# A store cut into pieces of 7, 70, 10, 40 and 1 rows, and VectorE's copies of V on later iterations

## The chip, the cores and the metric

The kernel runs on one core of one Trainium2 chip. The metric is the device time of one execution in microseconds (us). Times of a kernel are medians of several runs; a profile is one further execution, whose own time is given beside its span (first to last instruction of the program).

## The reference

Attention over 8 x 12 = 96 heads of 512 rows and 64 columns, float32 in and out. Each row attends to itself and to its ancestors in a binary tree whose node i has the parent (i - 1) // 2; everything else is masked.

```python
scores = np.einsum('bhqd,bhkd->bhqk', Q, K) * scale
scores = scores + (1 - mask) * (-1e9)
weights = np.exp(scores - np.max(scores, axis=-1, keepdims=True))
weights = weights / (np.sum(weights, axis=-1, keepdims=True) + 1e-10)
return np.einsum('bhqk,bhkd->bhqd', weights, V)
```

Q, K and V are 12.58 MB each, and so is the output.

## The kernel before

**Tiles.** The 96 heads are worked off in 48 pairs, one pair per iteration `i` of the loop at line 746 (49 iterations: the values and the division of pair `i - 1` run in iteration `i`). For a pair, TensorE transposes K and Q (`turn`, lines 427 and 459 for the wide form used from pair 8 on), VectorE copies the transposes out of PSUM (438, 442, 446 for K, 467 for Q; two pairs at a time, K in odd iterations and Q in even ones), TensorE makes the scores (`scores1`, `scores2`; the tree mask comes in as extra products with `codes`), ScalarE takes the exponential (502, 533), TensorE multiplies with V (`values`, 578), and VectorE takes the reciprocal of the sums (608) and multiplies (610) into the output tile `of`. In the wide form, the Q of pair `j` is transposed some two iterations before iteration `j`, its K some three.

**Loads.** Q, K and V come from HBM by DMAs that GpSimd (POOL) issues and that cast float32 to bf16. K and Q come in DMAs of up to 8 heads (`load_k`, `load_q`; line 253). V comes in groups of 16 heads: `load_rows` (line 282) brings 64 or 32 of the 128 partitions, `load_leaves` (line 291) brings the leaf rows of 8 heads to 32 partitions. Heads 48 to 63 are V's group 3, 64 to 79 group 4, 80 to 95 group 5.

**Copies of V.** Before V can be multiplied, its rows are copied within SBUF into `vt`, in the order of the tree (`spread`, the copy itself at line 361). There are two sets of `vt`, used by the groups in turn. The parts "A", "B", "C", "E" of groups 3 to 5 are the leaves and are copied by VectorE; "M" and "Y" of group 2 too; "X", "N", "Z0", "Z1" and the parts 6 to 9 (`spread_top`) of these groups are copied by POOL. Which engine copies what in which iteration is written out by hand: `BY_VECTOR` and `BY_SCALAR` by iteration, and from group 4 on `STEADY_VECTOR`, one copy in each iteration of the group before. The copy stands last in its iteration's work on VectorE. POOL's copy of "X" in group 2 needs VectorE's "M" of the same heads to have come first.

**Stores.** The output is stored from `of`, in tiles of 16 heads (`VO`): each of 128 partitions holds 1 KB for each head. Stores of heads 0 to 87 are issued by POOL, those of the last heads by SyncE (SP) and ScalarE (line 619 all).

**The order on POOL.** `pool_program` is one list of loads, copies and stores that POOL goes through in this order; `ready` only says from which iteration of the loop an entry may be emitted. Each DMA that POOL issues has one of eight semaphores in turn, and waits for the landing of the DMA that had it before, eight DMAs earlier in the list.

Of the kernel before, what the change touches and what calls it, by code (L numbers as in the profile page):

```python
# [119 lines left out]
def kernel(  # L120
# [7 lines left out]
    nc = tc.nc  # L128
    B, H, S, D = Q.shape
    P = nc.NUM_PARTITIONS  # L130
    assert S == 512 and D == 64 and P == 128 and (B * H) % 4 == 0
    scale = float(1.0 / np.sqrt(D))
    NH = B * H
# [3 lines left out]
    KB, VB, VO = 8, 16, 16  # L137
# [342 lines left out]
    def scores1(i):  # L480

        sp = psS.tile([P, 2, 512], fp32, name="s1")
        for a in range(2):
            nc.tensor.matmul(  # L484
                out=sp[:, a, :],
                lhsT=(k1code if i < WIDE else k1wide)[64 * a:64 * a + CODE_ROWS, :],
                rhs=(q1code[64 * a:64 * a + CODE_ROWS, :] if i < WIDE
                     else q1wide[64 * a:64 * a + CODE_ROWS, :, :]),
                start=True, stop=False,
            )  # L490
        for a in range(2):
            nc.tensor.matmul(  # L492
                out=sp[:, a, :], lhsT=keys(i, a, TOP),
                rhs=qTs[i][64 * a:64 * a + 64, :, :].rearrange("p t c -> p (t c)"),
                start=False, stop=True,
            )
        et = etpool.tile([P, 2, 4, 128], bf16, name="e1")
        nc.scalar.activation(  # L498
            out=et[:, :, :, :].rearrange("p a t c -> p (a t c)"),
            in_=sp[:, :, :].rearrange("p a c -> p (a c)"),  # L500
            func=AF.Exp, scale=scale,
        ) if i < WIDE else nc.scalar.activation(  # L502
            out=et[:, :, :, :].rearrange("p a t (r u) -> p a (t r) u", u=2),
            in_=sp[:, :, :].rearrange("p a (u c) -> p a c u", u=2),
            func=AF.Exp, scale=scale,
        )
        ets[i] = et
# [109 lines left out]
    def store(eng, h0, n, step=1, p0=0, p1=P):  # L617
        g, f = divmod(h0, VO)
        return eng.dma_start(  # L619
            out=Or[p0:p1, h0:h0 + step * (n - 1) + 1:step, :],  # L620
            in_=ofs[g][p0:p1, f:f + step * (n - 1) + 1:step, :, :].rearrange(
                "p h t d -> p h (t d)"
            ),
        )

    def pool_program():

        ops = [
            (load_k, 2, 2), (load_q, 2, 2), (load_v, 0, 4), (load_v, 4, 4),
            (load_k, 4, 2), (load_k, 6, 2), (load_q, 4, 2), (load_k, 8, 4),  # L630
            (load_q, 6, 2), (load_q, 8, 4), (load_v, 8, 8), (load_k, 12, 4),
            (load_q, 12, 4), (load_k, 16, 4), (load_rows, 1, "upper"),
            (load_q, 16, 4), (load_rows, 1, "even"), (load_k, 20, 4), (load_rows, 1, "odd"),
            (load_q, 20, 4), (load_k, 24, 8), (load_q, 24, 4), (load_rows, 2, "upper"),
            (load_q, 28, 4), (load_k, 32, 4), (load_rows, 2, "even", "odd"),
            (load_q, 32, 8), (load_k, 36, 4), (load_rows, 3, "upper"),
            (spread_pool, (1, "Z0", 8, 16), (1, "Z1", 8, 16)),
            (load_k, 40, 8), (load_q, 40, 8), (load_leaves, 3, 0), (load_leaves, 3, 1),
            (spread_top, 2, 0, 16), (spread_pool, (2, "Z0", 0, 16), (2, "Z1", 0, 16)),
            (load_q, 48, 8), (spread_pool, (2, "X", 0, 8)),  # L640
            (load_k, 48, 8), (spread_pool, (2, "X", 8, 16)),
            (load_rows, 4, "upper"), (spread_top, 3, 0, 16),
            (load_k, 56, 8), (load_q, 56, 8), (load_leaves, 4, 0), (load_leaves, 4, 1),
            (spread_pool, (3, "X", 0, 16), (3, "N", 0, 16), (3, "Z0", 0, 16), (3, "Z1", 0, 16)),
            (load_k, 64, 8), (load_q, 64, 8), (store, nc.gpsimd, 0, 16),
            (load_k, 72, 8), (spread_top, 4), (load_q, 72, 8),
            (spread_pool, (4, "X", 0, 16), (4, "N", 0, 16)),
            (load_rows, 5, "upper"), (spread_pool, (4, "Z0", 0, 16), (4, "Z1", 0, 16)),
            (load_leaves, 5, 0), (load_leaves, 5, 1), (load_k, 80, 8), (load_q, 80, 8),
            (store, nc.gpsimd, 16, 8), (load_k, 88, 8), (load_q, 88, 8),  # L650
            (store, nc.gpsimd, 24, 8), (store, nc.gpsimd, 32, 16),
            (spread_top, 5), (spread_pool, (5, "X", 0, 16), (5, "N", 0, 16)),
            (store, nc.gpsimd, 48, 16), (spread_pool, (5, "Z0", 0, 16), (5, "Z1", 0, 16)),
            (store, nc.gpsimd, 64, 8), (store, nc.gpsimd, 72, 8), (store, nc.gpsimd, 80, 8),
        ]
        return ops

    def ready(op, i):

        f, args = op[0], op[1:]  # L660
        if f in (load_k, load_q):
            return 2 * (i + 3) >= args[0] + args[1] - 4 * KB
        if f is load_v:
            return True
        if f in (load_rows, load_leaves):
            return 2 * i >= VB * (args[0] - 2)
        if f is spread_pool:
            tops = [(("vt", "M", VB * o + h) in issued) for o, part, h0, h1 in args if part == "X"
                    and o < EIGHT for h in range(h0, h1)]
            return 2 * i >= VB * (args[0][0] + 1 - NV) and all(tops)  # L670
        if f is spread_top:
            return 2 * i >= VB * (args[0] + 1 - NV)
        return 2 * i >= args[1] + args[2]

    BY_VECTOR = {
# [20 lines left out]
    }  # L696
    BY_SCALAR = {
# [8 lines left out]
    }  # L706

    STEADY_VECTOR = {
        0: [("A", 0, 8)], 1: [("B", 0, 8)], 2: [("C", 0, 8)], 3: [("E", 0, 8)],
        4: [("A", 8, 16)], 5: [("B", 8, 16)], 6: [("C", 8, 16)], 7: [("E", 8, 16)],  # L710
    }

    def spread_by(copy, table, steady, i):

        o, j = divmod(i, 8)
        todo = table.get(i, [])
        if 4 <= o + 1 < NH // VB:
            todo = todo + [(o + 1,) + piece for piece in steady.get(j, [])]
        for args in todo:
            spread(copy, *args)  # L720

    program = pool_program()

    def pool(i):
# [21 lines left out]
    for i in range(NP + 1):  # L746
        steps = FIRST[i] if i < len(FIRST) else "SVK" if i % 2 else "SVQ"
        for step in steps:
            if step == "S" and i < NP:
                scores1(i)  # L750
                scores2(i)
            if step == "V" and i >= 1:
                values(i - 1)
                norm(i - 1)
                valued = True
            if step == "K" and kdone < NP:
                kdone = turn("kst", kdone)
            if step == "Q" and qdone < NP:
                qdone = turn("qst", qdone)
            if step == "W":  # L760
                nc.scalar.copy(
                    out=codes[64:64 + CODE_ROWS, 1280:1536], in_=codes[0:CODE_ROWS, 1280:1536]
                )
            if step == "X":
                spin("s1" if valued else "ob", 2)
            if step == "D":
                spread_by(nc.vector.tensor_copy, BY_VECTOR, STEADY_VECTOR, i)
            if step == "A":
                spread_by(nc.scalar.copy, BY_SCALAR, {}, i)
        if "D" not in steps:  # L770
            spread_by(nc.vector.tensor_copy, BY_VECTOR, STEADY_VECTOR, i)
        if "A" not in steps:
            spread_by(nc.scalar.copy, BY_SCALAR, {}, i)
        pool(i)
        if i >= NP - 3 and i < NP:
            store(nc.sync, head(i - 1, 0), 2, 2)
# [33 lines left out]
```

## Time and profile before

| what | value |
| --- | --- |
| median of 3 runs | 135.08 us (134.81 to 135.19) |
| the profiled execution | 135.36 us |
| its span | 133.6 us |
| busy: PE, VectorE (DVE), ScalarE (ACT), POOL | 113.5, 108.0, 94.4, 73.5 us |
| DMAs issued by POOL, SP and ACT | 60, 6 and 3 |
| mean granted TensorE clock | 0.971 |

The profile's page shows each engine's busy time, the span in 40 slices (a slice here is 3.34 us; digits are tenths), the DMA queues, a chain of waits followed back from the last instruction, groups of instructions by line, and the DMA issues. Further views list an engine's instructions in order of time (start, length, engine, line, operation, output and inputs, shapes, count, and in brackets the idle time before it with what ended it), and the busy time of each engine in chosen stretches (from:to, length, then PE, PEld, DVE, ACT, POOL with instruction counts, then the granted clock, the mean busy share of the sixteen DMA engines, and GB/s). A DMA engine can have several packets open at once, so its share can be over 1. q0 is the queue of POOL's DMAs, q1 and q10 those of SP and ACT, q8 and q14 carry instructions. "DMA x<-y" as a releaser means that an engine waited for a DMA to land.

### The profile page before, as it was taken

The page shows a single profiled execution, that of the slowest core. Times are in us where ns is not written, and L with a number is a line of the kernel's source. Part 1 is how long each engine was busy: PE and PEld are TensorE (multiplying, and loading weights), DVE is VectorE, ACT ScalarE, POOL GpSimd, SP SyncE. Part 2 cuts the span into 40 slices and gives each one's busy share as a digit, 9 for nine tenths or more (in the row PEclk, how much of TensorE's full clock was granted, in tenths as well). Part 3 has the DMA queues.
Part 4 walks back from the last instruction along what each step waited for, and adds up shares of the span by engine and source line. Part 5 has one row for each costly group of instructions (what it writes and reads, how often), then busy time and mean ns, then how long its engine had stood idle before and what let it go on. Part 6 is the DMA issues. An engine that isn't in the chain of part 4 may idle for free.

```text
span 133.6 us, 5525 instructions
## 1 busy us (share of the span) xinstructions
PE 113.5 (85%) x2414; PEld 78.6 (59%) x2417; DVE 108.0 (81%) x261; ACT 94.4 (71%) x153; POOL 73.5 (55%) x98
## 2 busy tenths in 40 slices
PE   6887959999799799898899799999678998989910
PEld 2444646677577567575577567777456665666610
DVE  3349766888999999999999999995999998857440
ACT  4369575889769769686877858778567788696900
POOL 6999525364286996999705998223999302002000
PEclk9999995999999999999999999999999999999985
DMA  2999999999999999999999999999999999999980
GB/s 94 230 195 194 200 196 202 200 201 207 198 204 204 200 205 205 205 205 202 205 206 210 215 380 330 211 199 205 208 326 242 286 405 400 402 399 393 382 288 30
DMA packets 30232, 32.29 MB, mean 242 GB/s; under 512 B 1104, under 2 KB 27344, under 8 KB 30208
## 3 DMA queue, kind: packets, MB, share of 16 engines
q0 software_dynamic: 28352, 30.15, 113.0%
q1 hardware_dynamic: 1296, 1.33, 2.9%
q10 hardware_dynamic: 560, 0.46, 1.4%
q8 instruction: 19, 0.31, 0.9%
q14 instruction: 5, 0.04, 0.1%
HBM read 37.96 MB, written 12.58 MB: 378 GB/s over the span
## 4 chain that ended last, share of the span: by engine, by line
PE 30%; DVE 30%; DMA 18%; POOL 11%; issue 5%; ACT 2%; ACTq 0%; DVEq 0%; POOLq 0%
PE ob L578 11%; DVE of L610 10%; DMA vst<-in_V_dram 10%; DVE vt L361 8%; DMA kst<-in_K_dram 8%; PE s L484 4%; POOL vt L361 4%; DVE rec L608 3%; PE s L492 3%; DVE kq L467 3%; PE qtp L459 3%; PE ktp L427 3%; POOL kst L241 2%; POOL qst L241 2%; DVE kq L438 2%
## 5 line engine op out<-in xcount | busy, mean ns | idle before, releaser
L502 ACT ACTIVATE e<-s 128x1024 bf16<-128x1024 f32 x40 | 40.9, 1023 | 22.0 <-PE s L492 21.3
L578 PE MATMUL ob<-vt,e 128*128 128x65 bf16 (+1 forms) x940 | 37.4, 198 | 8.8 <-DVE of L610 5.8
L578 PEld LDWEIGHTS <-e 128*128 128x128 bf16 (+1 forms) x960 | 30.6, 103 | 17.8 <-DVE of L610 7.7
L533 ACT ACTIVATE e<-s 128x384 bf16<-128x384 f32 x80 | 34.7, 491 | 0.0
L610 DVE TENSOR_TENSOR of<-ob,rec 128x512 f32<-128x512 f32 x47 | 32.5, 691 | 1.6
L361 POOL COPY vt<-vst 32x512 int32<-32x512 int32 (+1 forms) x34 | 28.0, 823 | 7.6 <-PE ob L578 5.4
L361 DVE COPY vt<-vst 32x1024 bf16<-32x1024 bf16 (+6 forms) x54 | 26.3, 486 | 4.6 <-DMA vst<-in_V_dram 3.7
L484 PE MATMUL s<-codes 40*128 40x512 bf16 x96 | 19.3, 398 | 0.8 <-ACT e L498 0.4
L619 POOL DMA_DIRECT2D out_dram<-of x8 | 8.0, 997 | 20.1 <-DVE of L610 16.0
L492 PE MATMUL s<-kq 64*128 64x512 bf16 x96 | 18.5, 382 | 0.0
L608 DVE RECIPROCAL rec<-ob 128x8 f32<-128x8 f32 x47 | 9.6, 204 | 8.2 <-PE ob L578 7.6
L527 PEld LDWEIGHTS <-kq 64*128 64x128 bf16 x320 | 12.3, 94 | 5.6 <-issue 0.5
L527 PE MATMUL s<-kq 64*128 64x160 bf16 (+1 forms) x320 | 14.8, 208 | 0.3 <-issue 0.3
L517 PE MATMUL s<-codes 40*128 40x384 bf16 x80 | 13.6, 334 | 0.3
L467 DVE COPY kq<-qtp 128x1024 bf16<-128x1024 bf16 x20 | 13.6, 680 | 0.0
L427 PE MATMUL ktp<-ptile,kst 128*64 128x128 bf16 x320 | 12.5, 219 | 0.7 <-DVE kq L446 0.3
L498 ACT ACTIVATE e<-s 128x1024 bf16<-128x1024 f32 x8 | 8.2, 1022 | 6.3 <-PE s L492 6.3
L253 POOL DMA_DIRECT2D kst<-in_K_dram x12 | 9.0, 751 | 6.4 <-DMA kst<-in_K_dram 3.2
L459 PE MATMUL qtp<-ptile,qst 128*64 128x128 bf16 x320 | 12.3, 219 | 0.0
L253 POOL DMA_DIRECT2D qst<-in_Q_dram x12 | 8.8, 736 | 5.1 <-PE ob L578 2.1
L282 POOL DMA_DIRECT2D vst<-in_V_dram x9 | 6.8, 760 | 7.4 <-DMA vst<-in_V_dram 6.0
L517 PEld LDWEIGHTS <-codes 40*128 40x128 bf16 x80 | 5.8, 94 | 8.6 <-issue 1.3
(43 smaller groups left out, 124.3 us busy)
## 6 DMA issues: line engine op xcount, KB each, us to landing
out_dram<-of POOLq DMA_DIRECT2D x3, 2048.0 KB, 21.1
out_dram<-of POOLq DMA_DIRECT2D x5, 1024.0 KB, 17.0
kst<-in_K_dram POOLq DMA_DIRECT2D x8, 512.0 KB, 14.0
qst<-in_Q_dram POOLq DMA_DIRECT2D x8, 512.0 KB, 15.6
vst<-in_V_dram POOLq DMA_DIRECT2D x12, 256.0 KB, 13.7
vst<-in_V_dram POOLq DMA_DIRECT2D x6, 512.0 KB, 13.5
kst<-in_K_dram POOLq DMA_DIRECT2D x6, 256.0 KB, 11.9
qst<-in_Q_dram POOLq DMA_DIRECT2D x6, 256.0 KB, 12.2
```

What stands on the lines that cost most here:

```text
L253: return nc.gpsimd.dma_start(out=kept[b][:, h0 % KB:h0 % KB + n, :, :].rearrange("p (g x) t d -> p g (x t d)", x=2), in_=wide[:, h0 // 2:( ...
L361: return copy(out=dst, in_=src)
L427: nc.tensor.transpose(out=columns(kp[64 * a:64 * a + 64, :], mixed, (256, 2), (leaves - mixed, 2), (1, 32)), in_=st[:, 2 * i % KB // 2 + a ...
L467: nc.vector.tensor_copy(out=qq[:, :, 0:16, :].rearrange("p b u c -> p b (u c)"), in_=halves)
L484: nc.tensor.matmul(out=sp[:, a, :], lhsT=(k1code if i < WIDE else k1wide)[64 * a:64 * a + CODE_ROWS, :], rhs=(q1code[64 * a:64 * a + CODE_ ...
L492: nc.tensor.matmul(out=sp[:, a, :], lhsT=keys(i, a, TOP), rhs=qTs[i][64 * a:64 * a + 64, :, :].rearrange("p t c -> p (t c)"), start=False, ...
L502: ) if i < WIDE else nc.scalar.activation(
L517: nc.tensor.matmul(out=flat[:, a, :, :].rearrange("p u (t c) -> p u t c", t=4)[:, :, :, 16:64], lhsT=k2wide[64 * a:64 * a + CODE_ROWS, :], ...
L527: nc.tensor.matmul(out=flat[:, a, :, lo:hi], lhsT=keys(i, a, WTILE2[t]), rhs=qT[64 * a:64 * a + 64, :, lo:hi], start=False, stop=t == 1, s ...
L533: nc.scalar.activation(out=e2s[i % NE][:, a, :, 32:128].rearrange("p t (r u) -> p t r u", u=2), in_=flat[:, a, :, :].rearrange("p u (t r) ...
L578: nc.tensor.matmul(out=ob[lo:hi, a, 65 * t:65 * t + 65], lhsT=e[:, a, PLACE[t], lo:hi], rhs=vt[vtile[tile_v][0]][:, head(i, a) % VB, vtile ...
L610: nc.vector.tensor_tensor(out=ofs[g][:, first:last + 1:step, :, :], in0=o4[:, a:a + n, :, 0:D], in1=rec[:, a:a + n, :, :].to_broadcast([P, ...
```

## The change

`store_rows` cuts the store of heads 0 to 15 by partitions into five DMAs: rows 0 to 6, 7 to 76, 77 to 86, 87 to 126, and 127 (7, 70, 10, 40 and 1 rows of 16 heads each). The first two are issued between the loads of K and Q of heads 64 to 71, the third behind that load of Q, the last two behind POOL's copies 6 to 9 of group 4. Before, the whole store stood behind the load of Q of heads 64 to 71.

VectorE's copies of the leaves of groups 3, 4 and 5 are put in one table, one per iteration, from iterations 19, 27 and 35 on (before: group 3 two in each of the iterations 18, 20, 22, 24, groups 4 and 5 one per iteration from 24 and 32 on). In group 2, the two copies "M" and the first "Y" change places: "M" of heads 32 to 39 in iteration 13 (was 12), "Y" of the same in 14 (was 15), "M" of heads 40 to 47 in 15 (was 14). The number of copies stays. On POOL four DMAs are added.

```diff
+    DEALT = (0, 7, 77, 87, 127, P)
+
+    def store_rows(j0, j1):
+
+        for j in range(j0, j1):
+            store(nc.gpsimd, 0, VO, 1, DEALT[j], DEALT[j + 1])
+
     def pool_program():
...
-            (load_k, 64, 8), (load_q, 64, 8), (store, nc.gpsimd, 0, 16),
-            (load_k, 72, 8), (spread_top, 4), (load_q, 72, 8),
+            (load_k, 64, 8), (store_rows, 0, 2), (load_q, 64, 8), (store_rows, 2, 3),
+            (load_k, 72, 8), (spread_top, 4), (store_rows, 3, 5), (load_q, 72, 8),
...
+        if f is store_rows:
+            return 2 * i >= VO
...
-        12: [(2, "M", 0, 8)],
-        14: [(2, "M", 8, 16)],
-        15: [(2, "Y", 0, 8)],
+        13: [(2, "M", 0, 8)],
+        14: [(2, "Y", 0, 8)],
+        15: [(2, "M", 8, 16)],
         16: [(2, "Y", 8, 16)],
-        18: [(3, "A", 0, 8), (3, "B", 0, 8)],
-        20: [(3, "C", 0, 8), (3, "E", 0, 8)],
-        22: [(3, "A", 8, 16), (3, "B", 8, 16)],
-        24: [(3, "C", 8, 16), (3, "E", 8, 16)],
     }
+    for o, start in ((3, 19), (4, 27), (5, 35)):
+        for j in range(8):
+            h0 = VB // 2 * (j // 4)
+            BY_VECTOR[start + j] = [(o, "ABCE"[j % 4], h0, h0 + VB // 2)]
...
-    STEADY_VECTOR = {
-        0: [("A", 0, 8)], 1: [("B", 0, 8)], 2: [("C", 0, 8)], 3: [("E", 0, 8)],
-        4: [("A", 8, 16)], 5: [("B", 8, 16)], 6: [("C", 8, 16)], 7: [("E", 8, 16)],
-    }
-
-    def spread_by(copy, table, steady, i):
-
-        o, j = divmod(i, 8)
-        todo = table.get(i, [])
-        if 4 <= o + 1 < NH // VB:
-            todo = todo + [(o + 1,) + piece for piece in steady.get(j, [])]
-        for args in todo:
+    def spread_by(copy, table, i):
+
+        for args in table.get(i, []):
             spread(copy, *args)
```

More of the change, by code (lines that the diff above doesn't have):

```diff
@@ L766 @@
             if step == "D":
-                spread_by(nc.vector.tensor_copy, BY_VECTOR, STEADY_VECTOR, i)
+                spread_by(nc.vector.tensor_copy, BY_VECTOR, i)
             if step == "A":
-                spread_by(nc.scalar.copy, BY_SCALAR, {}, i)
+                spread_by(nc.scalar.copy, BY_SCALAR, i)
         if "D" not in steps:
-            spread_by(nc.vector.tensor_copy, BY_VECTOR, STEADY_VECTOR, i)
+            spread_by(nc.vector.tensor_copy, BY_VECTOR, i)
         if "A" not in steps:
-            spread_by(nc.scalar.copy, BY_SCALAR, {}, i)
+            spread_by(nc.scalar.copy, BY_SCALAR, i)
         pool(i)
```

## The prediction

> **What bounds the kernel now.** I read the page first (the slices by tenths, the DMA queues), then the busy time by stretches at the end, VectorE's timeline, and last the completion events of single DMAs.
>
> ```profile
> span 133.6 us, 5525 instructions
> DVE  3349766888999999999999999995999998857440
> DMA  2999999999999999999999999999999999999980
> GB/s 94 230 195 194 200 196 202 200 201 207 198 204 204 200 205 205 205 205 202 205 206 210 215 380 330 211 199 205 208 326 242 286 405 400 402 399 393 382 288 30
> q0 software_dynamic: 28352, 30.15, 113.0%
> q8 instruction: 19, 0.31, 0.9%
> q14 instruction: 5, 0.04, 0.1%
> HBM read 37.96 MB, written 12.58 MB: 378 GB/s over the span
> ```
>
> The DMA row stands at 9 from the second slice to the last but one: the sixteen DMA engines have work queued all the time, and the rate (a load counts its bf16 side here, so 205 GB/s is 410 read) moves little. The bytes are fixed. What can still differ is which engine ends last. The end:
>
> ```profile
> 126.00:127.00 1.00, 0.93 (x22) 0.67 (x21) 0.62 (x2) 0.92 (x3) 0.00 (x0) 1.00 1.00 377
> 129.50:130.00 0.50, 0.00 (x0) 0.00 (x0) 0.00 (x0) 0.00 (x0) 0.00 (x0) 0.50 0.83 289
> 130.00:130.50 0.50, 0.00 (x0) 0.00 (x0) 0.00 (x0) 0.00 (x0) 0.00 (x0) 0.50 0.34 105
> 130.50:131.00 0.50, 0.00 (x0) 0.00 (x0) 0.00 (x0) 0.00 (x0) 0.00 (x0) 0.50 0.21 68
> 131.00:131.50 0.50, 0.00 (x0) 0.00 (x0) 0.00 (x0) 0.00 (x0) 0.00 (x0) 0.50 0.20 70
> 131.50:132.00 0.50, 0.00 (x0) 0.00 (x0) 0.00 (x0) 0.00 (x0) 0.00 (x0) 0.50 0.06 21
> 128.75 0.35 ACTq L619 DMA_DIRECT2D out_dram<-of  x1
> ```
>
> The last but one column is the DMA share: 0.20 of sixteen is about three engines, alone at work from 130.5 to nearly 132. The last store is issued at 128.75. So the end is set by three late engines. Why they are late shows in the sixteen completion events that each DMA leaves, one for each engine (my own listing of the trace; the first column is the issue):
>
> ```
>  42.39 V leaves 3   55.9 56.2 56.3 56.4 56.4 56.4 56.8 56.9 57.4 57.4 57.4 57.5 57.6 57.6 57.6 57.9
>  51.30 V 4 upper    63.7 63.8 64.0 64.0 64.1 64.5 64.7 64.8 65.1 65.1 65.2 65.2 65.2 65.3 65.3 65.4
>  55.36 K 56 to 63   66.2 66.4 66.5 66.6 66.6 67.1 67.1 67.3 67.6 67.7 67.7 67.7 67.8 67.8 67.9 69.3
>  56.11 Q 56 to 63   68.7 68.9 69.1 69.1 69.1 69.6 69.7 69.8 70.2 70.2 70.2 70.3 70.4 70.4 70.5 71.4
>  62.61 K 64 to 71   73.8 74.0 74.2 74.2 74.3 74.7 74.8 74.9 75.3 75.3 75.3 75.4 75.5 75.5 76.5 76.6
>  63.36 Q 64 to 71   76.4 76.6 76.7 76.7 76.8 77.2 77.3 77.5 77.9 77.9 77.9 77.9 78.0 78.1 79.1 79.2
>  64.10 store 0-15   81.8 81.9 82.0 82.0 82.1 82.4 82.5 82.7 83.0 83.0 83.1 83.2 83.3 84.3 84.4 84.6
> 121.55 store 80-87 125.9 126.0 126.1 126.2 126.2 126.3 126.6 127.1 127.7 127.7 128.0 128.1 128.2 128.3 129.6 129.7
> 127.30 store 92,94 129.2 129.2 129.2 129.2 129.3 129.3 129.3 129.4 129.7 129.7 130.0 130.0 130.1 131.2 131.3 131.6
> 128.75 store 95    130.3 130.3 130.3 130.3 130.3 130.3 130.4 130.4 130.4 130.4 130.6 130.6 130.8 131.8 132.0 132.2
> ```
>
> Eight engines have fallen back by about 1.3 us at 65 us; then one, two and three of them fall back by another 1.1. The 19 instruction pieces of queue q8 explain it: 0.31 MB in 19 is 16 KB each, 0.9% of 16 engines x 133.6 us is 19 us, so 1.0 us on one engine each. Nineteen over eight engines in turn is two for each and a third for three of them. The other eight get none (a few have one of the short q14 pieces). That it is always the same eight is inferred from the steps in these rows.
>
> The computing ends beside this, and has one hole:
>
> ```profile
> 90.71 0.69 DVE L610 TENSOR_TENSOR of<-ob,rec 128x512 f32<-128x512 f32 x1
> 91.32 0.68 DVE L467 COPY kq<-qtp 128x1024 bf16<-128x1024 bf16 x1
> 93.64 0.62 DVE L361 COPY vt<-vst 32x1024 bf16<-32x1024 bf16 x1 [1.64 <-DMA vst<-in_V_dram]
> 96.11 0.85 DVE L361 COPY vt<-vst 32x1024 bf16<-32x1024 bf16 x1
> 98.55 0.92 DVE L361 COPY vt<-vst 32x1024 bf16<-32x1024 bf16 x1
> 101.44 0.42 DVE L361 COPY vt<-vst 32x1024 bf16<-32x1024 bf16 x1
> 103.46 0.67 DVE L361 COPY vt<-vst 32x1024 bf16<-32x1024 bf16 x1
> 95.41 4.96 POOL L361 COPY vt<-vst 32x512 int32<-32x512 int32 x6
> 101.52 2.33 POOL L361 COPY vt<-vst 32x1024 int32<-32x1024 int32 x2
> 111.07 0.69 DVE L610 TENSOR_TENSOR of<-ob,rec 128x512 f32<-128x512 f32 x1
> 112.72 0.21 DVE L608 RECIPROCAL rec<-ob 128x8 f32<-128x8 f32 x1 [0.36 <-PE ob L578]
> 124.77 0.69 DVE L610 TENSOR_TENSOR of<-ob,rec 128x512 f32<-128x512 f32 x1
> ```
>
> From 31 us VectorE hardly idles except for 1.64 us before 93.64, in front of the first copy of the V leaves of group 5; its copies take 0.62 to 0.92 beside POOL's copies and 0.42 alone. From 112 us it waits for PE.
>
> **The change, part by part. The store of heads 0 to 15.** One DMA of 128 rows is eight rows on each engine. Its 2.10 MB at about 401 GB/s (slices of 405, 400, 402) are 5.23 us, so 0.65 us for a row on one engine; the rows of Q 64 and of the store say the same (medians 77.7 and 82.85). The new pieces of 7, 70, 10, 40 rows don't divide by 16. No DMA of this kernel has such a number of rows, so how they fall is bounded. One end is an even spread by their 1 KB runs: eight rows' worth each, nothing moves. The other is whole rows on as many engines as divide the number, each piece starting where the last one stopped: 7 engines x 1, 14 x 5, 10 x 1, 10 x 4, and the last row in sixteen 1 KB runs. Counted from the first engine: places 0 to 4, 7 and 8 get ten rows, place 15 nine, places 5, 6 and 9 to 14 six. I take this end, because it splits the engines into eight that get more and eight that get less, as the rows above do, and four rows, 2.6 us, are near the 2.4 to 2.8 us between the first and the last engine there. The trace doesn't name the engines: whether the eight with six rows are the eight late ones is open, and is the first rival.
>
> Where they agree, the three last engines lose two rows: 132.24 - 1.31 = 130.9. The eight early ones gain two. They end 121.55's store at 125.9 to 127.1, and had they been kept fed, five more stores of 256, 256, 256, 128 and 128 KB (2.6 us at 401 GB/s) would end at 128.5 to 129.7; plus 1.31 is 129.8 to 131.0. The five in between come to 128.3 + 2.6 - 1.3 = 129.6. So the queue ends near 130.95 in place of 132.24: **-1.3 us**. Dealt without any rest, the mean over the engines, (8 x 129.0 + 5 x 130.6 + 3 x 132.1)/16 = 130.1, is the floor: -2.1 us.
>
> The Trainium skill ("DMA: Bandwidth & Descriptors", the section on why a DMA increments its semaphore by 16) states a division like the end I take: the largest number of engines up to 16 that divides the rows, then consecutive engines from a cursor. It also notes an exception, a sixteenth of the rows rounded up on each engine from the first, which is the second rival below. No run here shows either yet.
>
> **Four more DMAs on POOL, and three loads moved.** POOL's rows around them, and two of VectorE's:
>
> ```profile
> 51.30 0.83 POOL L282 DMA_DIRECT2D vst<-in_V_dram  x1
> 50.26 0.42 DVE L361 COPY vt<-vst 128x1024 bf16<-128x1024 bf16 x1
> 52.84 0.77 DVE L361 COPY vt<-vst 64x1024 bf16<-64x1024 bf16 x1
> 62.61 0.76 POOL L253 DMA_DIRECT2D kst<-in_K_dram  x1
> 63.36 0.75 POOL L253 DMA_DIRECT2D qst<-in_Q_dram  x1
> 64.10 1.18 POOL L619 DMA_DIRECT2D out_dram<-of  x1
> 65.92 0.75 POOL L253 DMA_DIRECT2D kst<-in_K_dram  x1 [0.64 <-PE s L492]
> 71.44 2.69 POOL L361 COPY vt<-vst 32x512 int32<-32x512 int32 x4 [4.77 <-PE ob L578]
> 74.09 0.74 POOL L253 DMA_DIRECT2D qst<-in_Q_dram  x1
> 80.18 1.15 POOL L291 DMA_DIRECT2D vst<-in_V_dram  x2
> 70.00:80.00 10.00, 8.93 (x206) 6.37 (x204) 9.64 (x23) 7.38 (x13) 8.21 (x10) 1.00 1.19 267
> ```
>
> Each issue costs POOL 0.58 (a load of 32 rows, two in 1.15) to 1.18; five in place of one are 1.7 to 4.7 us more, say 2.5. POOL idles 4.77 us before 71.44, which takes that. Each DMA also waits for the eighth one before it, so with four more in the row Q 64 to 71 goes out near 66 (behind V 4, 65.4), K 72 near 72 (Q 56, 71.4), Q 72 near 77 (K 64, 76.6), and the leaves of group 5, four copies later, near 83.5 in place of 80.18. Behind POOL then are its copies for group 4, wanted by PE at about 95. On the engines nothing runs dry: Q 64, issued at 63.36, lands at 76 to 79, so some 12 us lie queued, and the window has a share over 1. Cost 0; without that cover 2.5 to 3.3 us. Q 64 lands behind 77 rows of the store, 3.1 us later, at about 82; its transposes run two iterations before the copy of 91.32, near 87.
>
> The Trainium skill ("DMA: Bandwidth & Descriptors", "Rules for kernel authors") speaks against this: large DMAs of 128 partitions, small ones merged; with the 2.0 us of its fit ("Anatomy of one DMA") four more would cost 8 us, and the sum be 141.8, if they stood in line. The share over 1 says that they overlap instead.
>
> **VectorE's copies.** The same number, later: group 4 starts at iteration 27 (was 24), group 5 at 35 (was 32), each still ahead of the values of its heads (33 and 41). The 1.64 us wait goes, since iteration 35 is about 7 us later and the leaves have long landed. Four copies no longer run beside POOL: (0.62 + 0.85 + 0.92 + 0.67) - 4 x 0.42 = 1.38. Three copies of 0.42 move past 112 us into VectorE's gaps there. Together at most 4.3 us; the eight iterations between the L610 rows of 90.71 and 111.07 take 20.4, while the six from there to 124.77, where VectorE waits for PE, take 2.28 each; at that pace eight take 18.2, so about 2.1 is had, or 0 if PE gives nothing back. In group 2 one copy for POOL comes an iteration later (from 50.3 to 52.8), which moves the load of 51.30 by some 3 us, under the same backlog: 0. What is late next: the stores. Earlier computing feeds engines that are already fed, so its own worth at the end is **0** while the three late engines set it; it makes sure that the early ones don't rest after 127 us (share 0.67 there now).
>
> ```profile
> 127.00:128.00 1.00, 0.48 (x12) 0.32 (x10) 0.71 (x3) 0.00 (x0) 0.00 (x0) 1.00 0.67 245
> SPq L805 <- DMA out_dram<-of: 3.5, 1, 3.5
> ```
>
> **Sum.** The span's 133.6 less 1.3 is 132.3. The profiled execution took 135.36, so 1.76 lies around its span: 134.1. It stands 0.28 above the median of 135.08: **133.8 us**.
>
> **The rivals.** *The rows fall on the wrong engines* (slower): if one of the three late engines has ten rows, it ends at 132.24 + 1.31 = 133.55, and the whole at 136.4; with nine, 135.7. It decides from more than eight rows on any of the three. For it: nothing in the trace ties a row to an engine, and a blind fit is unlikely. Against it: the counts and the size match. *Rounded up from the first engine* (slower): pieces of 1, 5, 1 and 3 rows an engine give ten rows to seven engines, nine to three, eight to three, six to one, none to two; the three late ones then most likely have eight to ten: 135.1 to 136.4, say 135.9. *An even spread* (the change doesn't do what it says): the three late engines end at 132.2 as before, the computing's 2.1 us vanish behind them: 135.0. *Half a fit*, where the late ones lose one row: 134.4, which I count with the forecast.
>
> **How the numbers follow.** Forecast 0.60, wrong engines 0.22, rounded up 0.08, even spread 0.10. The three runs shown lie within 0.28%, so 0.3% (0.4 us) is about what can be told from no change. The forecast's own range is 133.0 (the floor) to 134.6; the slower cases reach 136.5. From 133.1 to 136.5 some 0.15 is left out. Faster 0.60, same 0.10, slower 0.30.
>
> **What would show it.** In the profile after: the DMA share in the last microsecond before the end falls from many engines at once, not in a step to three; the sixteen events of the DMAs after 82 us lie within about 1.5 us, where they lay 2.8 apart; no wait of VectorE for V at 93 us; the last copies at 0.42 and PE done near 125. Wrong would be a spread over 4 us after the store, a wait of VectorE or PE for Q 64, or a DMA share under 0.9 between 65 and 85 us.

## The result, and the profile after

| kernel | median | range, runs | ratio to before (95%) | profiled execution | its span |
| --- | --- | --- | --- | --- | --- |
| before | 135.08 us | 134.78 to 135.5, 10 | 1 | 135.36 us | 133.6 us |
| changed | 136.03 us | 135.53 to 137.16, 10 | 1.0079 (1.005 to 1.0109) | 136.0 us | 134.2 us |

The changed kernel is slower by 0.8%, where 133.8 us and faster was forecast. In the experiments a ratio is to the kernel before run beside it on the same chip (medians of 135.0 to 135.37 us). An execution more than 1.5% above the fastest of its kernel is left out of the ratios: one of 139.26 us of the pieces alone, and one of 146.06 us at a granted clock of 0.668 of the whole store issued earlier, which is also that kernel's only profile, so that of it only the times are used.

The page of the changed kernel, the lines that answer to those of before:

```profile
span 134.2 us, 5529 instructions
DVE  3439779888999899959999999898988999774400
DMA  4999999999999999999999999999999999999971
GB/s 132 212 176 195 199 196 200 201 202 206 200 201 203 202 204 206 206 207 201 209 202 211 311 247 243 255 221 201 207 311 257 278 382 402 403 404 398 401 284 48
q0 software_dynamic: 28624, 30.15, 113.4%
q8 instruction: 19, 0.31, 0.8%
```

The DMA row is the same as before, 9 from the second slice on, to the last but two. The hump of the store in the GB/s row (380, 330 before) is now spread over 311, 247, 243, 255. Nothing in these lines looks like a loss. It shows in the completion events (own listing: the issue, the first, the mean and the last of the sixteen events):

```
                       before                         changed
K 64 to 71   62.61  73.81  75.02  76.61     63.91  73.96  75.00  76.34
Q 72 to 79   74.09  86.77  88.05  89.94     76.82  86.63  88.96  92.50
Q 80 to 87   82.07  97.05  98.41  99.93     87.72  97.85  99.40 102.38
store 80-87 121.55 125.94 127.37 129.66    118.66 126.58 129.06 132.23
SP's last   128.20 129.71        131.93    125.31 128.49        133.32
ACT's last  128.75 130.29        132.24    125.86 128.84        132.59
```

Up to K 64 to 71, the last load ahead of the store, the two kernels agree within 0.3 us. Between it and Q 72 to 79 lie the same bytes in both (Q 64 to 71, the store of heads 0 to 15, K 72 to 79, Q 72 to 79). Before they took the sixteen engines 13.03 us on the mean, changed 13.96; and the engines lie 5.9 us apart behind them, where it was 3.2. The 2.6 us that the last engine loses (89.94 to 92.50) are still there at the store of heads 80 to 87 (129.66 to 132.23). The end, in stretches (the columns as in the prediction):

```profile
128.00:129.00 1.00, 0.00 (x0) 0.00 (x0) 0.00 (x0) 0.00 (x0) 0.00 (x0) 0.50 0.97 346
129.00:130.00 1.00, 0.00 (x0) 0.00 (x0) 0.00 (x0) 0.00 (x0) 0.00 (x0) 0.50 0.80 292
130.00:131.00 1.00, 0.00 (x0) 0.00 (x0) 0.00 (x0) 0.00 (x0) 0.00 (x0) 0.50 0.43 155
131.00:132.00 1.00, 0.00 (x0) 0.00 (x0) 0.00 (x0) 0.00 (x0) 0.00 (x0) 0.50 0.29 101
132.00:133.00 1.00, 0.00 (x0) 0.00 (x0) 0.00 (x0) 0.00 (x0) 0.00 (x0) 0.50 0.12 43
```

The share still falls in steps, to two engines in the last full microsecond, where it was to fall for many at once. The computing did end earlier, as the rows of VectorE, SP and ACT in order of time show:

```profile
91.39 0.69 DVE L610 TENSOR_TENSOR of<-ob,rec 128x512 f32<-128x512 f32 x1
93.09 0.42 DVE L361 COPY vt<-vst 32x1024 bf16<-32x1024 bf16 x1
95.41 0.70 DVE L361 COPY vt<-vst 32x1024 bf16<-32x1024 bf16 x1
97.99 0.40 DVE L361 COPY vt<-vst 32x1024 bf16<-32x1024 bf16 x1
123.87 0.73 PE L578 MATMUL s<-vt,e 128*64 128x65 bf16 x14
125.86 0.35 ACTq L619 DMA_DIRECT2D out_dram<-of  x1
```

No wait for V stands at 93 us, the copies take 0.40 to 0.42 but for one, PE ends at 124.6 and the last store is issued at 125.86 (before 128.75). And POOL's rows:

```profile
63.91 0.76 POOL L253 DMA_DIRECT2D kst<-in_K_dram  x1
64.67 1.62 POOL L619 DMA_DIRECT2D out_dram<-of  x2
66.47 0.79 POOL L253 DMA_DIRECT2D qst<-in_Q_dram  x1 [0.19 <-issue]
69.33 0.62 POOL L619 DMA_DIRECT2D out_dram<-of  x1 [2.07 <-DMA kst<-in_K_dram]
71.78 0.78 POOL L253 DMA_DIRECT2D kst<-in_K_dram  x1 [1.84 <-PE qtp L459]
75.42 1.41 POOL L619 DMA_DIRECT2D out_dram<-of  x2
76.82 0.82 POOL L253 DMA_DIRECT2D qst<-in_Q_dram  x1
82.91 0.59 POOL L291 DMA_DIRECT2D vst<-in_V_dram  x1
```

The five pieces take 1.62 + 0.62 + 1.41 = 3.65 where one took 1.18. So the pieces went out when they were to, the computing gained what it was to, and the DMA engines, busy all the time, did the same bytes in more time.

### The profile page after: what moved, and what is told of

The parts are those of the page before. It is cut to its first block, busy times and chain, and to the rows that moved or that the text cites. A ratio compares the mean times of both kernels' runs of the same rounds, so it can differ in the third digit from the quotient of the medians.

```text
span 134.2 us, 5529 instructions
## 1 busy us (share of the span) xinstructions
PE 113.0 (84%) x2414; PEld 78.6 (59%) x2417; DVE 106.6 (79%) x261; ACT 94.5 (70%) x153; POOL 76.4 (57%) x102
## 3 DMA queue, kind: packets, MB, share of 16 engines
q0 software_dynamic: 28624, 30.15, 113.4%
## 4 chain that ended last, share of the span: by engine, by line
PE 30%; DMA 30%; POOL 15%; DVE 11%; issue 5%; ACT 2%; ACTq 0%; POOLq 0%; DVEq 0%
DMA vst<-in_V_dram 16%; DMA qst<-in_Q_dram 13%; PE ob L578 10%; POOL vt L361 6%; PE s L484 5%; DVE vt L361 4%; PE qtp L459 3%; PE ktp L427 3%; DVE of L610 3%; PE s L492 3%; PE s L527 3%; PE s L517 2%; POOL kst L241 2%; POOL qst L241 2%; ACT e L533 1%
## 5 line engine op out<-in xcount | busy, mean ns | idle before, releaser
L361 DVE COPY vt<-vst 32x1024 bf16<-32x1024 bf16 (+6 forms) x54 | 24.7, 458 | 3.7 <-DMA vst<-in_V_dram 2.7
L619 POOL DMA_DIRECT2D out_dram<-of x12 | 10.4, 872 | 15.4 <-DVE of L610 10.4
L459 PE MATMUL qtp<-ptile,qst 128*64 128x128 bf16 x320 | 12.8, 220 | 1.5 <-issue 1.3
```

The source lines that it names most:

```text
L361: return copy(out=dst, in_=src)
L459: nc.tensor.transpose(out=halves[64 * a:64 * a + 64, :, c:c + 64], in_=st[:, 2 * i % KB // 2 + a, 4 * u + t, :], identity=ptile[:, 0:128],)
```

## The experiments

**The two parts alone.** First the new copies of VectorE with the store whole, then the pieces with the old copies.

```diff
 vec_only, against the changed kernel
-            (load_k, 64, 8), (store_rows, 0, 2), (load_q, 64, 8), (store_rows, 2, 3),
-            (load_k, 72, 8), (spread_top, 4), (store_rows, 3, 5), (load_q, 72, 8),
+            (load_k, 64, 8), (load_q, 64, 8), (store, nc.gpsimd, 0, 16),
+            (load_k, 72, 8), (spread_top, 4), (load_q, 72, 8),
 store_only: BY_VECTOR, STEADY_VECTOR and spread_by as before
```

> VectorE's copies moved as in the change, the store of heads 0 to 15 whole as before. Theory (the uneven pieces cost the time, through the DMA engine that ends last): the three late engines still end near 132.2 us, so 135.1 us (ratio 0.998 to 1.002), although the last store is issued 2 to 3 us earlier (near 126). Rival (moving the copies is what costs): 136.0 us, ratio 1.005 or more.

> The store cut into 7, 70, 10, 40 and 1 rows, VectorE's copies as before. Theory: about the changed kernel's time, 135.5 to 137.2 with the same wide scatter from run to run (ratio about 1.008), and completion events of one DMA up to 4 to 6 us apart after 82 us. Rival (moving the copies costs): 135.1 us.

Measured: VectorE's copies alone 134.76 us, ratio 0.9981 (0.9956 to 1.0006); the pieces alone 137.47 us, 1.0158 (1.0108 to 1.0209). From K 64 to Q 72 the mean is 13.07 and 14.14 us (13.03 before, 13.96 changed). The loss is the pieces'. VectorE's part is worth 0.3 us or nothing with the whole store, and about 1.1 us with the pieces (by the ratios, 1.0158 against 1.0079). In the run of the pieces alone the computing ends last, after one wait of 4.2 us of VectorE for V's leaves (until 95.84, when the slowest engine had brought them at 95.82):

```profile
DVE vt L361 <- DMA vst<-in_V_dram: 6.7, 4, 4.2
132.20 0.36 ACTq L619 DMA_DIRECT2D out_dram<-of  x1
```

**Even cuts.** The first theory was the dealing itself: whole rows in unequal numbers on the engines. Cut at 16, 80, 96 and 112 rows, every piece divides by 16 and each engine gets eight rows in all, as from the whole store.

```diff
-    DEALT = (0, 7, 77, 87, 127, P)
+    DEALT = (0, 16, 80, 96, 112, P)
```

> The changed kernel with the five pieces cut at 16, 80, 96, 112 (16, 64, 16, 16, 16 rows): five DMAs at the same places on POOL, but every one divides evenly over sixteen engines. Theory: 135.0 us (ratio 0.996 to 1.002), events after 82 us at most 3 us apart, little scatter. Rival (the five issues, their waits and the later loads cost): 136.0 us with the same scatter as the changed kernel.

Measured: 136.29 us, ratio 1.0088 (1.0057 to 1.0119), as slow as the changed kernel, and the mean from K 64 to Q 72 is 14.55 us, more than its 13.96. That theory fell. The time is that of the rival, that the five issues and the moved loads cost, which the cut by heads below puts to the test.

**A probe of the dealing.** The store of heads 32 to 47 was issued by SyncE in pieces of 64, five times 8, four times 4 and four times 2 rows, which was to name the engines.

```diff
-            (store, nc.gpsimd, 24, 8), (store, nc.gpsimd, 32, 16),
+            (store, nc.gpsimd, 24, 8),
...
+        if i == 24:
+            row = 0
+            for n in (64,) + (8,) * 5 + (4,) * 4 + (2,) * 4:
+                store(nc.sync, 32, 16, 1, row, row + n)
+                row += n
+            assert row == P
```

> A probe on the kernel before: heads 32 to 47 are stored from SyncE in one DMA of 64 rows, five of 8, four of 4 and four of 2, so that engines fixed by number get 4, 9, 13 and 17 rows (8, 4, 2 and 2 engines) if a piece of 8, 4 or 2 rows goes to that many lowest-numbered engines. Then the sixteen events of the next load fall in four sets 3.3, 2.6 and 2.6 us apart, and within each set the engines that carry the instruction pieces stand 1.2 to 2.4 us behind: this counts how many of the eight late engines are among numbers 0 to 1, 2 to 3, 4 to 7 and 8 to 15. If the late eight are not fixed engines, or pieces are spread evenly, no such sets appear. Time some 140 us, of no interest.

Measured: one execution, 141.9 us (span 140.1). The events of later loads lie up to 12 us apart, and they do fall in sets of 8, 4, 2 and 2: those of the load of Q issued at 95.82 us lie from 107.7 to 110.3, from 112.8 to 114.5, at 116.4 and 117.0, and at 118.7 and 119.8. This is what whole rows, on as many engines as the piece has rows, were to give. The means of the sets are 4.4, 2.9 and 2.6 us apart, where 3.3, 2.6 and 2.6 had been expected. How many of the late engines are in each set can't be read from them, so the question for the engines' names stays open. With some 140 us expected from the uneven dealing alone, the time speaks for no theory.

**Cut by rows in one place, cut by heads in five.** Two things were still mixed: that the store is cut by rows, and that it stands between loads in five places.

```diff
 together and even_together, against vec_only
-            (load_k, 64, 8), (load_q, 64, 8), (store, nc.gpsimd, 0, 16),
+            (load_k, 64, 8), (load_q, 64, 8), (store_rows, 0, 5),
 by_heads, against vec_only
-            (load_k, 64, 8), (load_q, 64, 8), (store, nc.gpsimd, 0, 16),
-            (load_k, 72, 8), (spread_top, 4), (load_q, 72, 8),
+            (load_k, 64, 8), (store, nc.gpsimd, 0, 1), (store, nc.gpsimd, 1, 9), (load_q, 64, 8),
+            (store, nc.gpsimd, 10, 1),
+            (load_k, 72, 8), (spread_top, 4), (store, nc.gpsimd, 11, 4), (store, nc.gpsimd, 15, 1),
+            (load_q, 72, 8),
 whole_earlier, against vec_only
-            (load_k, 64, 8), (load_q, 64, 8), (store, nc.gpsimd, 0, 16),
+            (load_k, 64, 8), (store, nc.gpsimd, 0, 16), (load_q, 64, 8),
```

> The changed kernel, with its five pieces of 7, 70, 10, 40 and 1 rows issued one after the other where the whole store stood (behind Q 64 to 71, ahead of K 72 to 79); VectorE's copies as in the changed kernel. Theory (turns: the DMA engines lose about 0.2 to 0.3 us each time the work changes between loads and a store, and the changed kernel has six such places where there were two): the cut alone costs nothing, 134.8 us as with VectorE's copies alone, and the engines' mean landing from K 64 to Q 72 is 13.0 to 13.3 us. Rival (few rows: a DMA of part of the rows uses few partitions at a time and runs slower wherever it stands): 136.0 to 136.5, mean 14.0 or more. Rival (uneven dealing by whole rows): 136.0 to 136.5 here, and 134.8 with the even cuts in the same place.

> The same place and the same number of pieces, cut at 16, 80, 96 and 112 rows, so that each engine gets eight rows of the store. Turns: 134.8 us, mean from K 64 to Q 72 13.0 to 13.3. Few rows: 136.0 to 136.5. Uneven dealing: 134.8, where the uneven pieces in this place would be slow.

> The store of heads 0 to 15 in five DMAs at the five places of the changed kernel, but cut by heads: 1, 9, 1, 4 and 1 heads, each of all 128 rows, so each engine gets eight rows of each. Turns: as slow as the changed kernel, 136.0 to 136.5 us, the mean from K 64 to Q 72 13.9 to 14.5. Few rows or uneven dealing: 134.8, mean 13.0 to 13.3.

> The whole store as one DMA, issued ahead of Q 64 to 71 in place of behind it (the place of the first two of the five pieces); VectorE's copies as in the changed kernel. Turns: as many as before, 134.8 us, mean from K 64 to Q 72 13.0 to 13.3. Rival (order: Q 64 to 71 behind store bytes makes the computing or a later load wait): 135.5 to 136.3, with a wait of TensorE or VectorE near 85 to 92 us.

Measured: together 137.12 us, 1.0155 (1.0127 to 1.0184); even and together 138.97, 1.0291 (1.0251 to 1.0331); by heads 134.74, 0.9976 (0.9958 to 0.9994); the whole store earlier 134.57, 0.9971 (0.9954 to 0.9989). The means from K 64 to Q 72 are 14.87, 15.17 and 12.98 us for the first three. The theory of turns fell on every count: five places cost nothing when every piece has all 128 rows, and one place costs more than five when the pieces have few. Uneven dealing fell again, since the even pieces are the slower ones here. What holds is the rival "few rows", though both kernels are above its 136.0 to 136.5 us; why pieces in one place cost more than in five was not tried.

**Which rows.** Few rows can be slow for three reasons: they sit in neighbouring SBUF partitions, they go to neighbouring rows of HBM, or any DMA of less than 128 rows is slow. Four kernels store heads 0 to 15 as two DMAs of 64 rows, in the place of the whole store, each engine getting four rows of each.

```diff
 against vec_only
-            (load_k, 64, 8), (load_q, 64, 8), (store, nc.gpsimd, 0, 16),
+            (load_k, 64, 8), (load_q, 64, 8), (store_half, 0), (store_half, 1),
+    def store_half(j):
+        sbuf, dram = ...
+        nc.gpsimd.dma_start(out=Or[dram, 0:VO, :], in_=ofs[0][sbuf, :, :, :]...)
 halves:         sbuf = dram = slice(64 * j, 64 * j + 64)
 odd_even:       sbuf = dram = slice(j, P, 2)
 halves_to_odd:  sbuf = slice(64 * j, 64 * j + 64), dram = slice(j, P, 2)
 odd_to_halves:  sbuf = slice(j, P, 2), dram = slice(64 * j, 64 * j + 64)
```

> VectorE's copies as in the changed kernel; the store of heads 0 to 15 in its old place, as two DMAs of 64 rows, the rows 0 to 63 and then 64 to 127. Every engine gets four rows of each, 1.05 MB a DMA. New theory (partitions: a store whose rows lie in neighbouring SBUF partitions is read through fewer paths out of the SBUF, where 128 rows, or every second row, reach all of them): slow, 136 to 140 us, the mean landing from K 64 to Q 72 at least 14 us where it is 13.0 with the whole store. Rival (memory: neighbouring rows in HBM are slow to write): slow as well. Rival (few: any DMA of less than 128 rows is slow): slow as well. Rival (uneven dealing or turns, both refuted by now): 134.7.

> The same two DMAs of 64 rows each, cut as the even rows 0, 2, ... 126 and the odd rows. Partitions: 134.7 us as the whole store, mean from K 64 to Q 72 13.0 to 13.4. Memory: 134.7 too. Few: as slow as the halves, 136 to 140.

> A probe: the SBUF rows 0 to 63 are written to the even rows of heads 0 to 15 in HBM and 64 to 127 to the odd ones, so these heads of the output are in another order. Partitions: slow as the halves, 136 to 140 us, mean 14 or more. Memory: 134.7, mean 13.0 to 13.4.

> The other probe: the even SBUF rows are written to rows 0 to 63 of heads 0 to 15 in HBM and the odd ones to 64 to 127, so these heads of the output are in another order. Partitions: 134.7 us, mean 13.0 to 13.4. Memory: slow as the halves, 136 to 140, mean 14 or more.

| SBUF rows of a DMA | HBM rows of a DMA | median | ratio (95%) | mean from K 64 to Q 72 |
| --- | --- | --- | --- | --- |
| 0 to 63, 64 to 127 | the same | 137.82 us | 1.0184 (1.0138 to 1.023) | 14.43 us |
| 0 to 63, 64 to 127 | even, odd | 137.29 us | 1.0146 (1.0111 to 1.0181) | 13.75 us |
| even, odd | the same | 134.99 us | 0.9983 (0.9962 to 1.0004) | 13.02 us |
| even, odd | 0 to 63, 64 to 127 | 134.94 us | 0.9965 (0.9934 to 0.9996) | 13.07 us |

The SBUF side decides: 2.3 to 2.9 us between the rows of the table that differ only in the partitions, about 0.5 us or less between those that differ only in the memory. (The mean of the second row, 13.75, is below the 14 that had been expected; its time is not.) The stretches over the store, of the contiguous halves, then of the even and odd rows:

```profile
78.00:80.00 2.00, 2.00 (x46) 1.33 (x43) 1.97 (x7) 1.69 (x4) 2.00 (x4) 1.00 1.04 373
80.00:82.00 2.00, 1.20 (x39) 1.05 (x39) 1.12 (x4) 1.67 (x3) 0.76 (x1) 1.00 1.00 307
82.00:84.00 2.00, 2.00 (x56) 1.43 (x52) 1.95 (x6) 1.14 (x3) 0.74 (x1) 1.00 1.06 233
84.00:86.00 2.00, 2.00 (x50) 1.43 (x45) 1.90 (x5) 1.70 (x4) 0.68 (x1) 1.00 1.14 172
86.00:90.00 4.00, 0.10 (x8) 0.02 (x1) 1.35 (x3) 0.87 (x3) 0.22 (x1) 0.91 1.28 192
```

```profile
78.00:80.00 2.00, 2.00 (x55) 1.44 (x52) 1.97 (x6) 1.18 (x2) 2.00 (x4) 1.00 1.05 400
80.00:82.00 2.00, 2.00 (x54) 1.46 (x50) 1.94 (x5) 1.70 (x4) 0.69 (x1) 1.00 1.03 373
82.00:84.00 2.00, 2.00 (x54) 1.45 (x50) 1.93 (x6) 1.67 (x4) 0.74 (x1) 1.00 1.20 257
84.00:86.00 2.00, 1.92 (x46) 1.29 (x41) 1.92 (x5) 1.69 (x4) 0.91 (x1) 1.00 1.25 208
86.00:90.00 4.00, 3.57 (x82) 2.52 (x82) 3.69 (x11) 2.70 (x6) 0.75 (x1) 1.00 1.35 200
```

The reader is to look at the last two columns together. The DMA share is 1.00 or more in both, so no engine lacks work; but 307 GB/s come out of it from 80 to 82 us in place of 373, and 172 in place of 208 four microseconds later. The packets themselves take longer (own listing, the 4 KB packets of the store begun in a stretch):

```
                  80 to 82 us        82 to 84 us
halves         142 of 203.5 ns     73 of 239.5 ns
even and odd   170 of 165.5 ns     48 of 165.0 ns
```

Over the whole store, the mean of its 4 KB packets parts the kernels (own listing). It is 163.8 to 164.7 ns before, with VectorE's copies alone, with the cut by heads and with both cuts into even and odd SBUF rows. It is 183.9 in the changed kernel, 180.1 with the pieces alone, 179.0 with even cuts, 200.3 and 214.7 with the pieces in one place (uneven and even), and 189.4 and 178.1 in the two kernels with SBUF rows 0 to 63 and 64 to 127. The medians are 159 to 165 in all of them, so some packets take much longer and most do not. In the changed kernel 19 ns more on some 32 packets of each engine are, as an estimate, 0.6 of the 0.93 us that the mean engine lost; the rest is not accounted for.

What this does to the rest is in PE's column: 0.10 of 4 us from 86 to 90. The slowest engine brings K 72 to 79 at 90.71 (86.87 with even and odd rows). POOL, whose next load waits for that landing, idles 5.0 us until 91.24. TensorE idles 4.46 us until 90.56:

```profile
POOL kst L253 <- DMA kst<-in_K_dram: 6.5, 2, 5.0
90.56 1.06 PE L427 MATMUL ktp<-ptile,kst 128*64 128x128 bf16 x16 [4.46 <-issue]
```

These transposes are those of heads 68 to 71, the fourteenth of twenty such groups, and their K had landed at 76.55; so it is not K that they wait for. "issue" means that the profile shows no releaser. What fits is TensorE's own instructions. It has 4,846 of them, and 0.31 MB over them are 64 bytes each, so the 19 pieces of queue q8 would be TensorE's, 256 instructions to a piece. By an own listing its instruction 3,009 begins at 80.80 us both with halves and with even and odd rows. The next piece begins at 88.31 and at 84.38, and instruction 3,265, the first of these transposes, at 90.56 and at 86.72: 2.25 and 2.34 us behind its piece, after 4.46 and 0.43 us of idling. With SBUF rows 0 to 63 to even HBM rows there are such stretches of 2.18, 0.97 and 1.64 us, each up to 2.5 us behind the start of a piece. The last stores of these two kernels are issued 4.9 and 5.2 us later than with even and odd rows, so most of what the halves cost in time seems to come this way. What held the pieces up, while the engines lay apart, the runs do not show. In the changed kernel no idling of this kind is over 0.7 us; there it is the late engines themselves that end last.

The Trainium skill ("SBUF — State Buffer", the section "Door 1: The DMA port swizzle") says that a transfer is limited by how many of 16 SBUF ports its partitions reach, and that rows 0 to 63 reach 8 of them, as rows 64 to 127 do. By its map every second row reaches all 16. Both agree with these four runs. Its rate for 8 ports, 218 GB/s, would make an estimate of 4.8 us for a half of 1.05 MB and 4.4 us more for the store; the mean engine lost 14.43 - 13.02 = 1.4 us. The runs do not show why it was less.

## Why the prediction was wrong

**What bounds the kernel.** The reading was that the engines always have work, that the bytes are fixed, and that "what can still differ is which engine ends last". The first two held. The third is the step that failed: a busy engine need not move bytes at a fixed rate. The whole stretch took 13.96 us in place of 13.03 on the mean, with the DMA row at 9 throughout.

**The store, -1.3 us.** The term took 0.65 us for a row on one engine from a store of 128 rows and used it for pieces of 7, 70, 10 and 40 neighbouring rows. That price holds for a piece whose partitions are spread over the SBUF (165 ns for each 4 KB packet with even and odd rows) and not for neighbouring ones (204 to 240 over most of the halves, 184 on the mean in the changed kernel). In place of -1.3, the last engine came 2.6 us later (store of heads 80 to 87), of which the end shows 132.24 to 133.32, 1.1 us, since the last stores are issued 2.9 us earlier. The dealing itself fits what was predicted: 28624 - 28352 = 272 packets more on q0 are 64 for the four more DMAs (the even cuts have just these), 12 for the last row in sixteen packets of 1 KB, and 196 of 16 bytes, which is 4 x (9 x 1 + 2 x 5 + 6 x 1 + 6 x 4): a short packet in place of each 4 KB one on the engines that get no rows, with 7, 14, 10 and 10 engines at work (four such packets to a row). Rows rounded up on each engine, the second rival, would make 132. Whether the six-row engines were the late ones stays open. It does not show in the time: even cuts, 136.29, and uneven ones, 136.03, have overlapping intervals.

**Four more DMAs, 0.** POOL's extra time of 2.5 us was right (2.47), and the issues near 66, 72, 77 and 83.5 us came at 66.47, 71.78, 76.82 and 82.91. The prediction's 5 us between the landing of Q 64 (82) and its transposes (87) were not there: it landed at 84.42, and the transposes of heads 64 to 67 began at 84.47, after 0.2 us of waiting. (The copy at 91.32 us, from which 87 was counted, belongs to heads 68 to 71; before, the transposes of heads 64 to 67 began at 85.45.) Even cuts have 1.6 us of idling there, and Q 64 at 84.64. It cost nothing at the end, for the last store goes out at 125.86 us in both. More DMAs and moved loads cost nothing, as the cut by heads shows with as many DMAs in the same places: 134.74. So the price by the number of DMAs that the prediction set beside it from the Trainium skill ("DMA: Bandwidth & Descriptors", "Anatomy of one DMA") has nothing in these runs to speak for it; the measured cost is that of the partitions.

**VectorE's copies.** The wait went, the copies but one are at 0.40 to 0.42, the last store went out 2.9 us earlier (2.1 had been estimated). Worth 0 at the end was right with the whole store: 0.9981, with an interval that holds 1. With the pieces it is worth about 1.1 us: with the old copies the computing waits for V that comes late and issues its last store at 132.20, with the new ones at 125.86.

**The rivals.** The time of the rival of the wrong engines, 136.4, is near what was measured, but its mechanism is not what happened: pieces that deal eight rows to every engine are as slow. None of the rivals had the partitions in it. Of the signs set down, the spread over 4 us after the store came (4.5 to 5.9), and the three signs of VectorE's part came as well. A wait of TensorE for Q 64 came too, of 0.2 us. A DMA share under 0.9 over the store did not come, so that sign could not have shown the loss.

The instruction pieces behind the three late engines are there as read: 19, of 0.89 to 1.01 us each in the changed kernel (own listing of q8). Before, those that begin at 67.3, 73.2 and 79.8 us are followed by one, two and three late events in the prediction's rows (69.3; 76.5 and 76.6; 84.3 to 84.6), which fits. That they make the engines late was not tested.

**A version that beats both.** VectorE's new copies with the whole store ahead of Q 64 to 71: 134.57 us, 0.9971 (0.9954 to 0.9989). Not much of it is the place, as VectorE's copies alone have 134.76.

## What to carry to other kernels

Cut a store by columns (here by heads) and keep all 128 partitions in each DMA; a store of neighbouring partitions alone takes more time for its bytes and pushes the engines apart for what comes behind it. Where it must be cut by rows, try every second one. A DMA share of 1 says that engines hold packets, not that they move bytes at full rate: compare GB/s, and the mean landing of the same bytes in both kernels. And what falls behind need not be the data: where TensorE idles with no releaser, compare with the instruction pieces. Before the price of a part is taken from the whole, ask whether the part reaches the same hardware.

## What the runs showed of the hardware

- Stores of 64 neighbouring partitions cost 2.3 to 2.9 us more in this kernel than the same stores of every second partition; where the rows lie in HBM made about 0.5 us at most. The mean 4 KB packet of the store takes 178 to 215 ns in the kernels cut into neighbouring rows, and 164 to 165 in those that are not.
- The loads of V do not show this. V 4 "upper", 64 neighbouring partitions and the same 1 MB read as a load of K, lands 2.7 us behind the load before it on the mean (62.0 to 64.7 us in the profile of before), and the next load of K 2.6 us later. A load writes bf16, half of what it reads, into the SBUF; whether that is the reason was not tried.
- TensorE's instructions seem to come through the same DMA engines, in pieces of 16 KB or 256 instructions, and it runs close behind them: with halves a piece that began 3.9 us later than with even and odd rows left it idle for 4.46 us.
- An engine that gets no rows of a DMA seems to get a 16-byte packet for each packet of a working engine's share. The trace has 196 of them, where before it has none; their count fits this, and they were not followed to their engines.
